# Two-layer gated-linear-attention and short-convolution trunk: the recurrence in 128-frame, two-head units with both chunks side by side on TensorE

## The chip, the cores and the metric

The kernel runs as one program on the 8 cores of one Trainium2 chip, one batch element a core. The metric is device time of the slowest core in microseconds (us). Every program here has a second, slower state: in some executions the cores of one die, or of both, get a lower granted TensorE clock and the time is some per cent longer. Below, "tile" means one pass of 512 frames through a mixer or a feed-forward; there are 8 of each in a layer and two layers, so 16 mixer tiles and 16 feed-forward tiles.

## The reference, cut to what matters

```python
def step(state, inp):                       # one chunk of 64 frames, 4 heads
    q_i, kd_i, v_i, g_i = inp
    state = g_i[..., None] * state + jnp.einsum('bhlk,bhlv->bhkv', kd_i, v_i)   # 128 x 256 a head
    o_i = jnp.einsum('bhlk,bhkv->bhlv', q_i, state)      # reads the state after its own chunk
    return state, o_i
# per layer
#   o   -> per-head RMSNorm, times silu(r), projection w_oa
#   conv: y_b = (gb_in * causal_depthwise_conv3(gc_in * cx)) @ w_ob
#   x  += (sigmoid(ga) * y_a + sigmoid(gb) * y_b) @ w_o
#   x  += SwiGLU(RMSNorm(x))
```

The state is float32. Shapes are x: 8 x 4096 x 1024; 4 heads with keys of 128 and values of 256; 64 chunks in sequence.

## The kernel before

A mixer tile computes q, k, v and the output gate, then runs the recurrence generator against the convolution generator, one step ("group") of each in turn. A group of the convolution is one accumulation of eight 128x512 matmuls, some 1.73 us, and the recurrence slips its small matmuls between them. 512 frames are four steps `ts` of 128 frames, each with two chunks `c`, nine groups a step.

```python
def AB(ts, c):                      # state matmuls of one chunk: all four heads, banks 2 and 3
    pr = slice(c * 64, (c + 1) * 64)
    for hp in range(2):
        mms([BK(2 + hp)], [... kd[pr, ts, head], v_s[pr, ts, head] ... for h2 in range(2)])
    for hh in range(4):             # VectorE: S = gamma * S + update, in place
        op("dve", [...], ["S32", ...], ... scalar_tensor_tensor(out=S32[:, hh, :], in0=S32[:, hh, :], ...))
    op("act", ["S32"], [("S16", si)], ...)          # ScalarE: one bf16 cast of all four heads
def C(ts, c): ...                   # output matmuls: q (64 frames) against the cast state
# E1: squares on ScalarE, rsqrt on GpSimd; E2: norm x gate on VectorE; Tr: eight transposes, two copies on VectorE
for ts in range(NTS):
    g = 9 * ts
    put(g, AB, ts, 0); put(g + 3, AB, ts, 1); put(g + 5, C, ts, 0); put(g + 6, C, ts, 1)
    put(g + 6, E1, ts); put(g + 9, E2, ts); put(g + 13, Tr, ts)
# ... (cut)
yield from interleave(gen_gla(), gen_conv(), [1])      # 41 groups of recurrence beside convolution
```

Beside a tile, the norm of the *next* tile starts a fixed number of groups in, and the weight casts to bf16 (DMAs that GpSimd issues, needed in the first layer for blocks of later stages) are paced by a rule:

```python
side += [lead(8), pre(), lead(8 if kind == "ffn" else 38), norm_h(s + 1)]
# ...
todo = casts.get(s, [])
ngroups = 52 if kind == "ffn" else 95
for _ in (mixer if kind == "mix" else ffn)(s):
    gi += 1
    next(sg, None)                                   # one step of the norm of the next tile
    while todo and gi * (len(casts[s]) + 1) > ngroups * (len(casts[s]) - len(todo) + 1):
        cast_piece(*todo.pop(0))
```

Of the kernel before, what the change touches and what calls it, by code (L numbers as in the profile page):

```python
# [12 lines left out]
KC = 8  # L13
# [112 lines left out]
def _mixer_blocks():  # L126

    c = _cols()
    w = lambda n, o, k: ("w_in", c[n] + o, k)
    bl = [("fzq", 8, 640, [w("fz", 0, 16)] * 8 + [w("q", 0, 512)])]  # L130
    bl += [("v0", 8, 512, [w("v", 0, 512)])]
    bl += [("k", 8, 512, [w("k", 0, 512)])]
    bl += [("v1", 8, 512, [w("v", 512, 512)])]
    bl += [("r%d" % h, 8, 512, [w("r", h * 512, 512)]) for h in range(2)]
    bl += [("cv%d" % i, 8, 640, [w(n, i * 128, 128) for n in ("C", "X", "B", "ga", "gb")]) for i in range(8)]
    bl += [("ab%d" % i, 8, 512, [(n, i * 256, 256) for n in ("w_oa", "w_ob")]) for i in range(4)]
    bl += [("o%d" % h, 8, 512, [("w_o", h * 512, 512)]) for h in range(2)]
    return bl
# [13 lines left out]
def build_nc(S):  # L152
# [19 lines left out]
    with ExitStack() as es:  # L172
# [9 lines left out]
        S32 = sb("S32", [128, 4, 256], F32)  # L182
        S16 = [sb("S16_%d" % i, [128, 4, 256], BF16) for i in range(2)]
        halo = sb("halo", [128, KC, 2], F32)
        gam = sb("gam", [128, 4, 2 * NTS], F32)
        ss = [sb("ss%d" % i, [128, 4], F32) for i in range(2)]
        rs2 = [sb("rs2_%d" % i, [128, 4], F32) for i in range(2)]
# [37 lines left out]
        ogtok = [carve([1024], BF16, "mix", [("og", i)]) for i in range(2)]  # L225
        ogT = carve([KC, T], BF16, "mix", R2("ogT", NTS, 2))
# [4 lines left out]
        ao[0] = span[("ogT", 0, 0)][1]  # L231
# [136 lines left out]
        def norm(xb, out_op):  # L368

            for j in range(4):  # L370
                i = min(j, 1)
                op("act", [("xT", xb, 2 * j), ("xT", xb, 2 * j + 1)], [("sq", i)],
                   lambda h, j=j, i=i: h.activation(out=sq[i][:], in_=xT[xb][:, 2 * j:2 * j + 2, :], func=AF.Square))  # L373
                if j:
                    op("dve", [("sq", 0), ("sq", 1)], [("sq", 0)],
                       lambda h: h.tensor_tensor(out=sq[0][:], in0=sq[0][:], in1=sq[1][:], op=ALU.add))  # L376
# [58 lines left out]
        def mixer(s):  # L435
# [6 lines left out]
            if t == 0:  # L442
                op("dve", [], ["S32"], lambda h: h.memset(S32[:], 0.0))
                op("dve", [], ["halo"], lambda h: h.memset(halo[:], 0.0))
# [79 lines left out]
            ei = 0  # L524
            for hf in range(2):
                sl, wk, w = get_block("r%d" % hf)
                for ts in range(NTS):
                    b = bank()
                    tm_group(b, w, wk, ts, h_, hk)
                    ei = 1 - ei  # L530
                    op("act", [BK(b)], ["eb%d" % ei], lambda h, b=b, ei=ei: h.activation(out=eb[ei], in_=pb[b][:, :], func=AF.Sigmoid))  # L531
                    op("dve", [BK(b), "eb%d" % ei], [("grs", ts, hf), BK(b)],
                       lambda h, b=b, ts=ts, hf=hf, ei=ei: h.tensor_tensor(out=grs[:, ts, hf * 512:(hf + 1) * 512], in0=pb[b][:, :], in1=eb[ei], op=ALU.mult))  # L533
                    yield
                done_block(sl)

            def gen_gla():
                s16c = [0]

                def AB(ts, c):  # L540
                    pr = slice(c * 64, (c + 1) * 64)
                    for hp in range(2):
                        ubk = 2 + hp
                        mms([BK(ubk)], [(mm(pb[ubk][:, h2 * 256:(h2 + 1) * 256], kd[pr, ts, (hp * 2 + h2) * 128:(hp * 2 + h2 + 1) * 128],
                                            v_s[pr, ts, (hp * 2 + h2) * 256:(hp * 2 + h2 + 1) * 256], True, True),
                                         [("kd", ts), ("v", ts, hp)]) for h2 in range(2)])
                    for hh in range(4):
                        ubk = 2 + hh // 2
                        op("dve", [BK(ubk), ("gam", hh)], ["S32", BK(ubk)],
                           lambda h, ubk=ubk, hh=hh, ts=ts, c=c: h.scalar_tensor_tensor(  # L550
                               out=S32[:, hh, :], in0=S32[:, hh, :], scalar=gam[:, hh, 2 * ts + c:2 * ts + c + 1],
                               in1=pb[ubk][:, (hh % 2) * 256:(hh % 2 + 1) * 256], op0=ALU.mult, op1=ALU.add))
                    si = s16c[0] % 2
                    s16c[0] += 1
                    op("act", ["S32"], [("S16", si)], lambda h, si=si: h.activation(out=S16[si][:], in_=S32[:], func=AF.Copy))  # L555

                def C(ts, c):
                    pr = slice(c * 64, (c + 1) * 64)
                    si = (ts * 2 + c) % 2
                    for hp in range(2):  # L560
                        mms([BK(hp)], [(mm(pb[hp][pr, (hh % 2) * 256:(hh % 2 + 1) * 256],
                                           qT[:, hh, ts * 128 + c * 64: ts * 128 + (c + 1) * 64], S16[si][:, hh, :], True, True),
                                        [("qT", hh), ("S16", si)]) for hh in (2 * hp, 2 * hp + 1)])

                def E1(ts):
                    r = ts % 2
                    for hh in range(4):
                        op("act", [BK(hh // 2)], ["junk", ("ss", r, hh)],
                           lambda h, hh=hh, r=r: h.activation(out=junk, in_=pb[hh // 2][:, (hh % 2) * 256:(hh % 2 + 1) * 256],  # L569
                                                              func=AF.Square, accum_out=ss[r][:, hh:hh + 1]))  # L570
                    op("pool", [("ss", r, hh) for hh in range(4)], [("rs2", r)],
                       lambda h, r=r: h.tensor_scalar(out=rs2[r][:], in0=ss[r][:], scalar1=1.0 / 256, scalar2=EPS, op0=ALU.mult, op1=ALU.add))
                    op("pool", [("rs2", r), "mhalf"], [("rs2", r)],
                       lambda h, r=r: h.tensor_tensor(out=rs2[r][:], in0=rs2[r][:], in1=mhalf[:, 0:4], op=ALU.pow))

                def E2(ts):
                    r = ts % 2
                    for hh in range(4):
                        op("dve", [BK(hh // 2), ("rs2", r), ("grs", ts, hh // 2)], [("og", r), BK(hh // 2)],
                           lambda h, hh=hh, r=r, ts=ts: h.scalar_tensor_tensor(  # L580
                               out=ogtok[r][:, hh * 256:(hh + 1) * 256], in0=pb[hh // 2][:, (hh % 2) * 256:(hh % 2 + 1) * 256],
                               scalar=rs2[r][:, hh:hh + 1], in1=grs[:, ts, hh * 256:(hh + 1) * 256], op0=ALU.mult, op1=ALU.mult))

                def Tr(ts):
                    r, tb = ts % 2, 2
                    tb16 = pb[tb][:, :].bitcast(BF16)
                    mms([BK(tb)], [(lambda pe, vc=vc: pe.transpose(tb16[:, vc * 128:(vc + 1) * 128], ogtok[r][:, vc * 128:(vc + 1) * 128], ident16[:]),  # L587
                                    ["ident16", ("og", r)]) for vc in range(8)])
                    for par in range(2):
                        src = tb16.rearrange("p (a b c) -> p a b c", a=4, b=2)[:, :, par, :]  # L590
                        dst = ogT[:, :, ts * 128:(ts + 1) * 128].rearrange("p (a b) c -> p a b c", b=2)[:, :, par, :]
                        op("dve", [BK(tb), "pk"], [("ogT", ts, par), BK(tb)],
                           lambda h, src=src, dst=dst, par=par: h.tensor_scalar_mul(out=dst, in0=src, scalar1=pkc(96 + l * 2 + par)))
# [4 lines left out]
                for ts in range(NTS):  # L598
                    g = 9 * ts
                    put(g, AB, ts, 0)  # L600
                    put(g + 3, AB, ts, 1)
                    put(g + 5, C, ts, 0)
                    put(g + 6, C, ts, 1)
                    put(g + 6, E1, ts)
                    put(g + 9, E2, ts)
                    put(g + 13, Tr, ts)
                for g in range(41):
# [4 lines left out]
            def gen_conv():  # L612
                for cc in range(8):
# [9 lines left out]
                    op("act", ["halo"], [("ub", u)], lambda h, u=u, cc=cc: h.activation(out=ub[u][:, 0:2], in_=halo[:, cc, :], func=AF.Copy))  # L623
                    op("dve", [BK(b), ("tmp", u)], [("ub", u), BK(b)],
                       lambda h, b=b, u=u, csb=csb: h.tensor_tensor(out=ub[u][:, 2:T + 2], in0=pb[b][:, :], in1=csb[:], op=ALU.mult))  # L625
                    op("act", [("ub", u)], ["halo"], lambda h, u=u, cc=cc: h.activation(out=halo[:, cc, :], in_=ub[u][:, T:T + 2], func=AF.Copy))
                    cw = lambda j, cc=cc: pkc(32 + (l * 3 + j) * 8 + cc)
                    op("dve", [("ub", u), "pk"], [("tmp", 2 + u)],
                       lambda h, u=u, cc=cc, cw=cw, cacc=cacc: h.tensor_scalar(out=cacc[:], in0=ub[u][:, 2:T + 2], scalar1=cw(2), scalar2=pkc(80 + l * 8 + cc),  # L629
# [208 lines left out]
```

## Time and profile before

The median was 4867.46 us (4866.63, 4867.46 and 5444.5). The profile is of a run of 4876.38 us; its slowest core, core 3, spans 4875.2 us. A table of the stages of that core, from the starts of successive tiles:

| stage, core 3 | us |
|---|---|
| before the first mixer tile | 31.1 |
| first mixer tile | 217.7 |
| mixer tiles 1 to 7, layer one | 1318.3 |
| mixer tiles, layer two | 1448.4 (180.9 each in the steady state) |
| 16 feed-forward tiles | 1860.0 |

The profile names engines PE (TensorE matmuls), PEld (its weight loads), DVE (VectorE), ACT (ScalarE), POOL (GpSimd) and SP. `L324` is a line of the kernel; most matmuls come through one helper and share that line, so a matmul is told by its tiles. A number in square brackets after a timeline entry is the idle time of that engine before it, and after the arrow stands what ended the idle time. What ended an idle time is inferred by the profiler's reader from semaphore events, and can be wrong.

### The profile page before, as it was taken

The numbers are of one execution on the slowest core, as the hardware profiler recorded it, in microseconds if no ns is written. First come the engines' busy times: TensorE is split into PE (matmuls) and PEld (weight loads), VectorE is DVE, ScalarE is ACT, GpSimd is POOL, SyncE is SP. The second block draws the span as 40 slices with busy tenths as digits, with TensorE's granted clock in tenths as the row PEclk, the third lists the DMA queues.
The fourth block names the chain that finished last, engine by engine and source line by source line (L and its number), as shares of the span: only waits on it lengthen the run. The fifth ranks groups of instructions, "written<-read, shape, count | busy, mean of one in ns | idle before, by whom it ended". The sixth has DMA issues, their size and how long they took to land.

```text
span 4875.2 us, 62749 instructions; the slowest of 8 cores (4823.3 to 4875.2 us)
## 1 busy us (share of the span) xinstructions
PE 4664.7 (96%) x21840; PEld 2092.2 (43%) x21840; DVE 2173.2 (45%) x3425; ACT 1348.2 (28%) x2479; POOL 130.1 (3%) x210
## 2 busy tenths in 40 slices
PE   6899899999999999999999999999999999999998
PEld 2334344444444444444444444444444444444443
DVE  3535545645545222222235545546645633333332
ACT  2232323323322111211123323323323312222221
POOL 0000000000000000000000000000000000000000
PEclk9989999999999999999999999999999999999999
DMA  9975674584775755566554464454454455555552
GB/s 208 227 197 164 149 207 160 145 205 151 184 203 188 225 192 192 183 195 197 183 177 155 146 197 169 140 190 159 139 186 168 131 213 188 191 186 190 182 186 90
DMA packets 124195, 870.18 MB, mean 178 GB/s; under 512 B 14480, under 2 KB 14608, under 8 KB 47504
## 3 DMA queue, kind: packets, MB, share of 16 engines
q1 hardware_dynamic: 116928, 782.29, 46.9%
q0 software_dynamic: 5952, 81.27, 11.0%
q8 instruction: 182, 2.98, 0.2%
q10 hardware_dynamic: 1008, 2.62, 0.2%
q14 instruction: 125, 1.02, 0.1%
HBM read 856.94 MB, written 148.37 MB: 206 GB/s over the span
## 4 chain that ended last, share of the span: by engine, by line
PE 81%; DVE 7%; DMA 6%; issue 3%; ACT 2%; DVEq 0%; ACTq 0%; POOL 0%; SPq 0%; POOLq 0%
PE pb L324 78%; DMA sb_wsl<-sc_mix_cv 3%; DVE sb_S L550 2%; PE pb L336 2%; DMA sb_wsl<-w_mix 1%; DVE sb_arena L580 1%; ACT sb_sq L373 1%; DVE sb_tmp L633 1%; DVE sb_ub L625 1%; ACT sb_arena L569 1%; PE pb L587 1%; DMA sc_mix_cv<-sb_wsl 1%; DVE sb_tmp L629 1%; DVE sb_sq L376 0%; DMA sc_mix_k<-sb_wsl 0%
## 5 line engine op out<-in xcount | busy, mean ns | idle before, releaser
L324 PE MATMUL pb<-sb_hT,sb_wsl 128*128 128x512 bf16 x8768 | 2030.2, 389 | 40.4 <-DMA sb_wsl<-sc_mix_cv 30.3
L324 PEld LDWEIGHTS pb<-sb_hT,sb_wsl 128*128 128x128 bf16 x8768 | 848.9, 100 | 1119.8 <-issue 226.0
L324 PE MATMUL pb<-sb_arena,sb_wsl 128*128 128x512 bf16 x3836 | 837.2, 379 | 2.0 <-DMA sb_wsl<-w_mix 1.9
L324 PE MATMUL pb<-sb_hT,sb_arena 128*128 128x512 bf16 x3136 | 683.2, 379 | 0.0
L704 ACT ACTIVATE sb_tmp<-pb 128x512 f32<-128x512 f32 x352 | 209.8, 596 | 1300.6 <-PE pb L324 1255.4
L324 PEld LDWEIGHTS pb<-sb_arena,sb_wsl 128*128 128x128 bf16 x3836 | 374.3, 98 | 452.2 <-issue 5.0
L709 DVE TENSOR_TENSOR sb_arena<-pb,sb_tmp 128x512 bf16<-128x512 f32 x352 | 242.8, 690 | 683.5 <-PE pb L324 614.2
L324 PE MATMUL pb<-sb_arena 128*128 128x512 bf16 (+1 forms) x2052 | 420.7, 355 | 83.2 <-DVE sb_S L550 83.2
L324 PEld LDWEIGHTS pb<-sb_hT,sb_arena 128*128 128x128 bf16 x3136 | 307.2, 98 | 374.0 <-issue 7.4
L324 PE MATMUL pb<-sb_wsl,sb_hT 128*128 128x512 bf16 x2048 | 460.3, 384 | 4.6 <-DMA sb_wsl<-w_mix 4.6
L419 DVE TENSOR_TENSOR sb_xT<-pb,sb_xT 128x512 f32<-128x512 f32 x256 | 171.1, 689 | 648.2 <-PE pb L324 567.5
L324 PEld LDWEIGHTS pb<-sb_arena 128*128 128x128 bf16 (+1 forms) x2052 | 188.1, 97 | 329.4 <-issue 144.0
L324 PEld LDWEIGHTS pb<-sb_wsl,sb_hT 128*128 128x128 bf16 x2048 | 200.6, 99 | 245.1 <-issue 27.0
L550 DVE SCALAR_TENSOR_TENSOR sb_S<-sb_S,sb_gam,pb 128x256 f32<-128x256 f32 x512 | 245.0, 478 | 64.6 <-ACT sb_S_0 L555 22.3
L495 ACT ACTIVATE sb_arena<-pb 128x512 bf16<-128x512 f32 x64 | 36.2, 590 | 734.2 <-PE pb L324 734.2
L633 DVE SCALAR_TENSOR_TENSOR sb_tmp<-sb_ub,sb_pk,sb_tmp 128x512 f32<-128x512 f32 x256 | 192.3, 751 | 27.4 <-DVE sb_tmp L629 0.5
L625 DVE TENSOR_TENSOR sb_ub<-pb,sb_tmp 128x512 f32<-128x512 f32 x128 | 88.3, 690 | 253.9 <-ACT sb_ub L623 130.8
L376 DVE TENSOR_TENSOR sb_sq<-sb_sq 128x1024 f32<-128x1024 f32 x120 | 147.0, 1225 | 118.4 <-ACT sb_sq L373 96.9
L373 ACT ACTIVATE sb_sq<-sb_xT 128x1024 f32<-128x1024 f32 x160 | 166.7, 1051 | 104.5 <-DVE sb_sq L376 81.4
L401 DVE SCALAR_TENSOR_TENSOR sb_hT<-sb_xT,sb_pk,sb_rstd 128x512 bf16<-128x512 f32 x256 | 175.5, 745 | 31.5 <-ACT sb_rstd L386 31.5
L640 ACT ACTIVATE sb_arena<-pb 128x512 bf16<-128x512 f32 x256 | 148.4, 588 | 56.5 <-PE pb L324 55.9
L533 DVE TENSOR_TENSOR sb_arena<-pb,sb_arena 128x512 bf16<-128x512 f32 x128 | 87.1, 691 | 163.3 <-ACT sb_arena L531 159.2
(77 smaller groups left out, 2392.5 us busy)
## 6 DMA issues: line engine op xcount, KB each, us to landing
sb_wsl<-sc_mix_cv SPq DMA_DIRECT2D x120, 1280.0 KB, 7.2
sb_arena<-sc_ffn_f SPq DMA_DIRECT2D x98, 1024.0 KB, 5.7
sb_wsl<-sc_ffn_f SPq DMA_DIRECT2D x78, 1024.0 KB, 6.0
sb_wsl<-sc_mix_ab SPq DMA_DIRECT2D x60, 1024.0 KB, 5.0
sb_arena<-sc_ffn_d SPq DMA_DIRECT2D x70, 704.0 KB, 4.6
xs<-sb_xT SPq DMA_DIRECT2D x48, 1024.0 KB, 4.7
sb_xT<-xs SPq DMA_DIRECT2D x96, 512.0 KB, 8.3
sb_wsl<-sc_ffn_d SPq DMA_DIRECT2D x58, 704.0 KB, 4.8
```

The costliest lines, as they stand in the source:

```text
L324: return lambda pe: pe.matmul(out, lhsT, rhs, start=first, stop=last)
L336: ins = e.h.matmul(pb[b][:, :], w[:, kc, col0:col0 + 128], rhsT[:, kc, :], start=(kc == 0), stop=(kc == KC - 1))
L373: lambda h, j=j, i=i: h.activation(out=sq[i][:], in_=xT[xb][:, 2 * j:2 * j + 2, :], func=AF.Square))
L376: lambda h: h.tensor_tensor(out=sq[0][:], in0=sq[0][:], in1=sq[1][:], op=ALU.add))
L401: lambda h, kc=kc: h.scalar_tensor_tensor(out=hT[xb][:, kc, :], in0=xT[xb][:, kc, :], scalar=pkc(g0 + kc), in1=rstd[:], op0=ALU.mult, op1= ...
L419: lambda h, b=b, dc=dc: h.tensor_tensor(out=xT[xb][:, dc, :], in0=pb[b][:, :], in1=xT[xb][:, dc, :], op=ALU.add))
L550: lambda h, ubk=ubk, hh=hh, ts=ts, c=c: h.scalar_tensor_tensor(out=S32[:, hh, :], in0=S32[:, hh, :], scalar=gam[:, hh, 2 * ts + c:2 * ts + ...
L625: lambda h, b=b, u=u, csb=csb: h.tensor_tensor(out=ub[u][:, 2:T + 2], in0=pb[b][:, :], in1=csb[:], op=ALU.mult))
L633: lambda h, u=u, cw=cw, j=j, cacc=cacc: h.scalar_tensor_tensor(out=cacc[:], in0=ub[u][:, j:T + j], scalar=cw(j), in1=cacc[:], op0=ALU.mult ...
L640: lambda h, b=b, dst=dst, cc=cc: h.activation(out=dst[:, cc, :], in_=pb[b][:, :], func=AF.Sigmoid))
L704: lambda h, b=b, si=si: h.activation(out=tmp[si][:], in_=pb[b][:, :], func=AF.Silu))
L709: lambda h, b=b, si=si, fc=fc: h.tensor_tensor(out=hid[:, fc, :], in0=pb[b][:, :], in1=tmp[si][:], op=ALU.mult))
```

## The change

Its intent: take the recurrence's small matmuls closer together and its waits apart. The unit becomes 128 frames and two heads. Both chunks of a unit are issued alternately: state matmuls on TensorE's upper and lower 64 rows, output matmuls on its left and right 64 columns. Two are meant to run at once; for the column halves no run had shown it yet. A unit comes every six groups, 52 groups in all, and the output gate's projection and half of the convolution's output projection join the convolution as filler. The state alternates between two float32 buffers. Transpose copies and the first convolution tap go from VectorE to ScalarE, the halo copies from ScalarE to GpSimd. The norm of the next tile starts four groups earlier, and its four squares get one more group each (an added `yield`), so that its root and its multiplications still come at the same group count of the tile.

```diff
+                def AB(u):
+                    ts, hp = u // 2, u % 2
+                    mms([BK(0), BK(1)], [(mm(pb[c][:, h2 * 256:(h2 + 1) * 256],
+                                             kd[c * 64:(c + 1) * 64, ts, (hp * 2 + h2) * 128:(hp * 2 + h2 + 1) * 128],
+                                             v_s[c * 64:(c + 1) * 64, ts, (hp * 2 + h2) * 256:(hp * 2 + h2 + 1) * 256], True, True),
+                                          [("kd", ts), ("v", ts, hp)]) for h2 in range(2) for c in range(2)])
 ... (four state updates on VectorE, S32[c] -> S32[1 - c])
+                def SC(u):            # one bf16 cast on ScalarE per chunk, two heads
+                def C(u):             # four output matmuls, h2 outer, c inner, one bank; squares, rsqrt
-                for ts in range(NTS):
-                    g = 9 * ts
-                    put(g, AB, ts, 0)
 ... (cut)
+                for u in range(8):
+                    for d, st in ((0, AB), (1, SC), (3, C), (6, E2), (9, Tr)):
+                        put(6 * u + d, st, u)
+                for g in range(52):
 ... (convolution)
-                    op("act", ["halo"], [("ub", u)], ... halo copy in ...)
+                    op("pool", [("halo", cc)], [("ubh", u)], ... halo copy in ...)
-                    op("dve", [("ub", u), "pk"], [("tmp", 2 + u)], ... first tap ...)
+                    op("act", [("ub", u), "pk"], [("tmp", 2 + u)], ... first tap ...)
 ... (cut)
+            def main():
+                yield from gen_r()
+                yield from gen_conv()
+                yield from gen_ob(0)
-            yield from interleave(gen_gla(), gen_conv(), [1])
+            yield from interleave(gen_gla(), main(), [1])
 ... (cut)
-                side += [lead(8), pre(), lead(8 if kind == "ffn" else 38), norm_h(s + 1)]
+                side += [lead(8), pre(), lead(8 if kind == "ffn" else 34), norm_h(s + 1)]
 ... (in the norm, after each of the four squares)
+                yield
```

## The prediction

> **What bounds the kernel now.** I read the summary of engines first, then TensorE's waits, then the timeline of one undisturbed mixer tile, then stretches.
>
> ```profile
> PE 4664.7 (96%) x21840; PEld 2092.2 (43%) x21840; DVE 2173.2 (45%) x3425; ACT 1348.2 (28%) x2479; POOL 130.1 (3%) x210
> ```
>
> TensorE is the bound; the other engines matter only where they make it wait. Of its matmuls, 19840 are bf16 with 512 columns. At full clock they start 215.8 ns apart in the trace, so they cost 19840 x 0.2158 = 4281 us, and the change touches none of them. A stretch of a feed-forward tile shows that floor with nothing on top:
>
> ```profile
> core 7: us, PE busy (x) PEld busy (x) DVE busy (x) ACT busy (x) POOL busy (x), PEclk, DMA share, GB/s
> 1550.00:1663.00 113.00, 113.00 (x524) 51.19 (x522) 29.36 (x41) 22.31 (x31) 0.58 (x1) 1.00 0.73 247
> ```
>
> Differences between the starts of successive tiles put the 16 feed-forward tiles together at 1860.0 us on all eight cores, the 16 mixer tiles at 2934 to 2984 us, with 31 us ahead of the first mixer. In the second layer every mixer tile takes 180.8 to 181.0 us on every core. The waits say what is in a mixer beyond matmuls (us in total, times, longest):
>
> ```profile
> PE pb L324 <- DVE sb_S L550: 83.2, 35, 12.3
> PE pb L587 <- DVE sb_S L550: 34.9, 19, 2.3
> PE pb L324 <- DMA sb_wsl<-sc_mix_cv: 30.3, 5, 9.9
> PE pb L324 <- DVE sb_sq L379: 28.9, 2, 21.0
> ```
>
> The first two, 118 us, are the recurrence: a matmul needs a PSUM bank that VectorE's state update (L550) has not yet emptied, or a transpose needs the normalised output. The fourth is 21 us of start and 8 us of the last norm. One second-layer tile of core 7 in TensorE's timeline:
>
> ```profile
> 2898.82 1.90 PE L324 MATMUL pb<-sb_hT,sb_wsl 128*128 128x512 bf16 x8
> 2903.01 1.00 PE L587 MATMUL pb<-sb_ident,sb_arena 128*128 128x128 bf16 x8 [2.29 <-DVE sb_S L550]
> 2903.80 3.21 PE L324 MATMUL pb<-sb_hT,sb_wsl 128*128 128x512 bf16 x8
> ...
> 2934.62 5.35 PE L324 MATMUL pb<-sb_hT,sb_wsl 128*128 128x512 bf16 x24
> 2943.64 0.38 PE L324 MATMUL pb<-sb_arena 64*128 64x256 bf16 x2 [3.67 <-DVE sb_S L550]
> 2944.81 0.58 PE L324 MATMUL pb<-sb_arena 64*128 64x256 bf16 x2 [0.79 <-DVE sb_S L550]
> 2945.32 3.60 PE L324 MATMUL pb<-sb_hT,sb_wsl 128*128 128x512 bf16 x8
> ```
>
> Each tile has two stalls, at the first output transpose and where the last 128 frames meet the next tile's norm on VectorE, 6.7 us together; after each, eight matmuls take 3.2 to 3.6 us instead of 1.9, because the clock was halved. The first tile has another limit:
>
> ```profile
> 60.00:110.00 50.00, 42.15 (x198) 18.25 (x195) 15.97 (x26) 16.07 (x32) 2.11 (x4) 0.97 1.01 231
> 180.00:230.00 50.00, 45.55 (x209) 20.36 (x208) 29.81 (x46) 5.50 (x16) 3.92 (x6) 0.97 1.01 218
> ```
>
> The last two numbers are the share of the DMA engines and GB/s (core 3): weights are read, cast and stored there, and the queues are full. Later mixer tiles of core 7 have shares of 0.54 to 0.69.
>
> [...] the four forget-gate matmuls of 16 rows start 7 ns apart, and their eight f32 passes occupy about 1.07 us together. No run here shows it for column groups yet. [...] a full matmul followed by a 64-row one is 311 ns from start to start instead of 215, and the first full one after a 64-row one comes 202 ns after its start instead of 109. [...] the change gives the two chunks banks 0 and 1. [...]
>
> **The change part by part, for a steady mixer tile.**
>
> *Pairing.* Before, eight calls of four state matmuls (64 rows, 256 columns) cost 311 - 216 = 95 ns to enter, 3 x 109, and 202 to leave: 0.62 us each, and eight output calls (64 columns) the same: 94 + 327 + 205 = 0.63. After, there are again eight of each with four matmuls, but alternating between two groups, so a call is two rounds of 109 instead of four: about 95 + 218 + 93 + some 10 ns = 0.42 us. Saving 0.21 x 16 = 3.3 us a tile. The mode switches stay; the 32 transposes stay at 56 ns.
>
> *The recurrence's stalls.* Before, 128 frames pass in nine groups, state steps three groups apart, each step updating four heads (4 x 0.478 us) in two banks that the next step needs. The recurrence is spread over 41 groups with convolution alone, whose VectorE work I sum per tile as 32 x 0.478 updates, 16 x 0.482 gates, 8 x 0.482 transpose copies, 8 x (0.690 + 0.547 + 2 x 0.751 + 0.686) convolution and 10 us of norm: 65 us of some 81 without stalls. After, a unit comes every six groups (6 x 1.73 = 10.4 us plus about 1.1 of its own), and transpose copies and the first tap go to ScalarE: 52 groups hold some 65 us of VectorE work, the output gates' products and four more included, in about 97 us. The state banks have six groups to be emptied, not three. State values alternate between two buffers, so an update no longer waits for the cast of the one before.
>
> The tightest path left is state matmul to output matmul, three groups apart, about 5.6 us. In it: a leftover convolution operation, at worst two taps until 1.4 us; two output gates, to 2.5; four updates at 0.58 spacing, to 4.7; the second half-size cast, to some 5.4 (estimated 0.63 from 1.06 for the double size). So it just fits, and with a norm addition (1.23 us) inside it misses by about a microsecond. I allow 1.5 us of small stalls a tile[...].
>
> *Halo copies to GpSimd.* VectorE waited 130.8 us in total for ScalarE's tiny copy of the two carried frames (L623), which stood behind state casts in ScalarE's order. That wait leaves with its order; it was one source of the stalls above, so I count it once.
>
> *Sum.* 712 x 0.2158 = 153.7; state and output calls 16 x 0.42 = 6.8; output transposes 1.8; key transposes 0.9; forget gate 1.2; norm sum 0.9. That is 165.3, plus 1.5: 166.8 us against 180.8, or 14 less: 3.3 of pairing, 6.7 of stalls less the 1.5 that remain, and the rest, about 5.5, the halved clock after them and smaller waits.
>
> *First layer.* The first tile, 209 to 218 us, is full of DMA; its 12.35 us stall comes from GpSimd, which stood at a weight load (behind the store of an earlier block) with the normalisation behind it. That order stays, now with the halo copies behind it too. I keep 213. Tiles 1 to 7 stall up to 9.9 us for a convolution block, when casts for later layers share the DMA engines. Those loads stay. Convolution blocks will be used up every 9.4 us instead of 11, so I keep 40 us for these seven tiles rather than the 35 that core 7 shows.
>
> Total: 31 + 213 + (7 x 166.8 + 40) + (8 x 166.8 + 2) + 1860 = 4648 us in the profile. The timed runs were 9 us below the profile before (4867 against 4876), so 4640.
>
> **Rivals.** (1) *Column groups do not overlap*: half of the pairing goes, 8 x 0.21 x 16 = 27 us more, 4667. For it: narrow weight loads average 112 ns in the trace, longer than the 98 of full ones, and nothing before shows two column groups together. Against it: loads overlap matmuls everywhere else. (2) *The wait only moves*: output matmuls or transposes wait for casts on ScalarE, which now also has copies and the first tap (estimate 128 x 0.6 + 256 x 0.38 = 174 us more on 1348), or VectorE waits for GpSimd. At 3 us a tile with a halved clock behind it, that is 16 x 5 = 80 us more, 4720. For it: the tight path above and table loads of 1.28 us around the norm. Against it: ScalarE stays near 1500 us. (3) *DMA becomes the bound in the first layer*: blocks come late at the faster pace; 7 x 5 = 35 us more, 4675. Against it: shares of 0.54 to 0.69. (4) *All stalls vanish*, first tile included: 4640 - 24 - 25 = about 4590.
>
> **Range and chances.** Pairing and stalls would both have to fail for 2% (97 us) to be missed; even rival 2 leaves 3%. The range goes from just above rival 4 to short of rival 2: 4598 to 4700. Faster by over 2%: 0.97; within 2%: 0.025; slower: 0.005.
>
> **What would show it.** In the profile after: feed-forward tiles unchanged; second-layer mixer tiles at 165 to 169 us; VectorE state waits on TensorE below 40 us in total instead of 118; four state matmuls in about 0.3 us from first start to last end of streaming, and a few nanoseconds between starts of a pair, also for the column pairs; less half clock than the 215 us of core 3 before; convolution-block waits still there. It would be wrong if second-layer tiles stay above 172 us, with a wait on casts (ScalarE) or on GpSimd in place of L550.

## The result, and the profile after

The changed kernel is correct. Its first four runs took 4721.24 us (fast) and 5055.97, 5084.69 and 4960.37 us (slow), two more 4729.34 us (fast) and 5074.42 us (slow). The ratio of fast runs to those of before is 0.971 (95% interval 0.9682 to 0.9738): faster, by 141 us. Ratios here and below are the mean time of one kernel's fast runs over that of the other's of the same rounds, so not quite the ratio of the medians quoted. The kernel was run again later (see the experiments): 4719.62, 4723.27 and 4726.6 us, ratio 0.9705. The profile is of the run of 4721.24 us, and the sums below are against it: the predicted 4640 us is 81 us too low, and the range ended 21 us below it.

The summary of engines and TensorE's waits after (core 3, the slowest; us in total, times, longest) answer to the first and third fence of the prediction:

```profile
PE 4549.9 (96%) x21840; PEld 2035.9 (43%) x21840; DVE 2026.7 (43%) x3169; ACT 1535.9 (33%) x2735; POOL 226.3 (5%) x594
```

```profile
PE pb L324 <- DMA sb_wsl<-sc_mix_cv: 47.3, 7, 11.0
PE pb L324 <- DVE sb_sq L380: 29.4, 2, 21.4
PE pb L324 <- ACT sb_S_2 L561: 21.5, 16, 1.4
PE pb L591 <- DVE sb_arena L582: 18.5, 19, 14.0
PE pb L324 <- DMA sb_wsl<-w_mix: 18.2, 11, 2.8
PE pb L324 <- ACT sb_S_3 L561: 11.6, 16, 1.0
```

The 83.2 + 34.9 us of waits on VectorE's state update (L550 before) are gone. In their place stand waits on ScalarE's cast of the last unit (sb_S_2 and sb_S_3, L561): 21.5 and 11.6 us, each sixteen times, that is once in every mixer tile. The convolution block wait grew from 30.3 to 47.3 us.

The pairs do overlap. Four output matmuls of one call in the timeline (start, duration, engine, line, tiles):

```profile
1024.19 0.30 PE L324 MATMUL pb<-sb_S_0,sb_arena 128*64 128x256 bf16 x1
1024.20 0.30 PE L324 MATMUL pb<-sb_S_1,sb_arena 128*64 128x256 bf16 x1
1024.33 0.27 PE L324 MATMUL pb<-sb_S_0,sb_arena 128*64 128x256 bf16 x1
1024.33 0.27 PE L324 MATMUL pb<-sb_S_1,sb_arena 128*64 128x256 bf16 x1
```

The two chunks (S_0 and S_1) start within 10 ns of each other, and the second pair 130 ns later. The starts of a state call pair in the same way: at the median 3 ns between the two starts of a pair and 116 ns from pair to pair (core 3). Medians over all calls, from the start of the matmul before the call to the start of the one after it, less the time that its kind takes from start to start (0.216 us, after a transpose 0.056), are 0.42 us for a state call and about 0.44 for an output call, against 0.64 and 0.65 before.

A steady mixer tile of the second layer takes 170.3 us, against 180.9 before and 166.8 predicted. What keeps it above 166.8 is one place in the tile. Core 3, timeline, cut to what leads to the wait:

```profile
3028.81 1.28 ACT L386 ACT_TABLE_LOAD   x1
...
3030.84 0.69 DVE L623 TENSOR_TENSOR sb_ub<-pb,sb_tmp 128x512 f32<-128x512 f32 x1 [2.65 <-ACT sb_rstd L386]
...
3031.42 1.02 ACT L597 ACTIVATE sb_arena<-pb,sb_pk 128x256 bf16<-128x256 bf16 x2
...
3033.28 0.80 ACT L627 ACTIVATE sb_tmp<-sb_ub,sb_pk 128x512 f32<-128x512 f32 x1
...
3034.87 1.61 DVE L633 SCALAR_TENSOR_TENSOR sb_tmp<-sb_ub,sb_pk,sb_tmp 128x512 f32<-128x512 f32 x2 [1.84 <-POOL sb_ub L621]
...
3036.40 2.73 DVE L402 SCALAR_TENSOR_TENSOR sb_hT<-sb_xT,sb_pk,sb_rstd 128x512 bf16<-128x512 f32 x4
3039.05 1.07 DVE L582 SCALAR_TENSOR_TENSOR sb_arena<-pb,sb_rs_0,sb_arena 128x256 bf16<-128x256 f32 x2
...
3040.03 1.05 DVE L552 SCALAR_TENSOR_TENSOR sb_S_1<-sb_S_0,sb_gam,pb 128x256 f32<-128x256 f32 x2
...
3041.18 0.63 ACT L561 ACTIVATE sb_S_2<-sb_S_1 128x512 bf16<-128x512 f32 x1 [4.71 <-DVE sb_S_1 L552]
...
3041.95 0.27 PE L324 MATMUL pb<-sb_S_2,sb_arena 128*64 128x256 bf16 x1 [1.42 <-ACT sb_S_2 L561]
...
3042.93 0.27 PE L324 MATMUL pb<-sb_S_3,sb_arena 128*64 128x256 bf16 x1 [0.70 <-ACT sb_S_3 L561]
...
3043.24 5.09 PE L324 MATMUL pb<-sb_hT,sb_wsl 128*128 128x512 bf16 x15
```

Read from the top. The norm of the next tile (its table load of 1.28 us, L386, L387, and its multiplications L402) meets the last unit of the recurrence. The first idle time of VectorE, 2.65 us, is put down to the norm's root (L386), but that is a coincidence of times: L623 does not read the root, and it started 0.18 us after its own convolution group had ended on TensorE, as 80 of the 128 L623 of this core did. VectorE merely had no work. The second is real: 1.84 us for the halo copy of GpSimd (L621), which comes behind two small operations (L574, L576) that wait for ScalarE's squares, and these stand behind the norm's root on ScalarE. Then the convolution taps, four norm multiplications (2.73 us) and two output gates all go ahead of the state updates, which begin at 3040.03. The state matmuls had been issued at 3034.05, so the updates come 6 us after them, and the casts behind: ScalarE had stood idle for 4.71 us until the update came. TensorE loses 1.42 + 0.70 us, and the chunks of this unit run one after the other instead of in pairs. Behind it the clock is halved (granted 0.50 from 3043.25 to 3046.66): 15 matmuls take 5.09 us, where at 0.2158 us a start they would take about 3.4. The stretches of that tile (us, busy time and count of each engine, granted clock, DMA share, GB/s) put a size to it:

```profile
2923.50:3093.90 170.40, 168.01 (x836) 75.05 (x835) 91.90 (x150) 71.43 (x137) 12.41 (x34) 0.99 0.54 175
3041.90:3050.00 8.10, 7.34 (x28) 3.02 (x29) 4.19 (x7) 4.69 (x11) 1.06 (x3) 0.79 0.01 2
```

TensorE idles 170.40 - 168.01 = 2.4 us in the tile, and in the 8.1 us around the wait the mean clock of 0.79 costs 8.1 x 0.21 = 1.7 us more. With the pairing that this one call lost, these are most of the 4.9 us by which the tile stands above the 165.4 that experiments below reach. The record holds a check of the 1.7 us: on every core one second-layer tile takes 168.6 or 168.7 us instead of 170.3, and on core 3 (its tile 2) that one has the same waits of 1.42 and 0.70 us (2873.36 and 2874.33) and no halved clock: the granted clock is 1.00 from 2868 to 2876, and the 24 matmuls behind take 5.35 us. The other seven second-layer tiles of that core each have one stretch of half clock, 3.41 us long. What spared the eighth is not shown; the same stall cost 2.1 us there and about 3.8 in the others.

In the first layer, tiles 1 to 7 of core 3 took 180.0, 180.2, 173.8, 170.9, 181.8, 180.4 and 181.9 us: 57 us above seven steady ones. The first tile took 216.5 us and the feed-forward tiles 1860.1. The sum is 31.5 + 216.5 + 1249.0 + 1363.1 + 1860.1 = 4720.2 us.

### The profile page after: what moved, and what is told of

It is laid out like the page before. It is cut to its first block, busy times and chain, and to the rows that moved or that the text cites.

```text
span 4720.2 us, 63804 instructions; the slowest of 8 cores (4686.8 to 4720.2 us)
## 1 busy us (share of the span) xinstructions
PE 4549.9 (96%) x21840; PEld 2035.9 (43%) x21840; DVE 2026.7 (43%) x3169; ACT 1535.9 (33%) x2735; POOL 226.3 (5%) x594
## 2 busy tenths in 40 slices
DMA packets 124202, 870.25 MB, mean 184 GB/s; under 512 B 14480, under 2 KB 14608, under 8 KB 47504
## 4 chain that ended last, share of the span: by engine, by line
PE 85%; DMA 9%; DVE 2%; ACT 2%; issue 1%; POOL 0%; ACTq 0%; DVEq 0%; POOLq 0%; SPq 0%
PE pb L324 83%; DMA sb_wsl<-sc_mix_cv 4%; DMA sb_wsl<-w_mix 3%; PE pb L336 2%; DVE sb_hT L402 1%; DMA sc_mix_cv<-sb_wsl 1%; ACT L386 0%; PE pb L591 0%; DMA sc_mix_r<-sb_wsl 0%; DMA sc_mix_fzq<-sb_wsl 0%; DMA sc_mix_oa<-sb_wsl 0%; DVE sb_S_1 L552 0%; DVE sb_S_0 L552 0%; DVE sb_tmp L633 0%; ACT sb_arena L571 0%
## 5 line engine op out<-in xcount | busy, mean ns | idle before, releaser
L324 PE MATMUL pb<-sb_hT,sb_wsl 128*128 128x512 bf16 x8768 | 1983.5, 384 | 60.4 <-DMA sb_wsl<-sc_mix_cv 47.3
L725 DVE TENSOR_TENSOR sb_arena<-pb,sb_tmp 128x512 bf16<-128x512 f32 x352 | 243.3, 691 | 783.2 <-PE pb L324 652.1
L324 PE MATMUL pb<-sb_arena 128*128 128x512 bf16 (+1 forms) x2052 | 386.8, 353 | 0.0
L324 PEld LDWEIGHTS pb<-sb_arena 128*128 128x128 bf16 (+1 forms) x2052 | 165.1, 97 | 232.4 <-issue 49.6
L402 DVE SCALAR_TENSOR_TENSOR sb_hT<-sb_xT,sb_pk,sb_rstd 128x512 bf16<-128x512 f32 x256 | 177.9, 746 | 31.7 <-ACT sb_rstd L387 30.1
L623 DVE TENSOR_TENSOR sb_ub<-pb,sb_tmp 128x512 f32<-128x512 f32 x128 | 88.3, 690 | 224.4 <-PE pb L324 139.6
L647 DVE TENSOR_TENSOR sb_arena<-pb,sb_tmp 128x512 bf16<-128x512 f32 x128 | 88.0, 687 | 166.8 <-PE pb L324 166.8
L597 ACT ACTIVATE sb_arena<-pb,sb_pk 128x256 bf16<-128x256 bf16 x256 | 119.9, 469 | 112.8 <-PE pb L591 100.7
```

What stands on the lines that cost most here:

```text
L324: return lambda pe: pe.matmul(out, lhsT, rhs, start=first, stop=last)
L402: lambda h, kc=kc: h.scalar_tensor_tensor(out=hT[xb][:, kc, :], in0=xT[xb][:, kc, :], scalar=pkc(g0 + kc), in1=rstd[:], op0=ALU.mult, op1= ...
L597: lambda h, src=src, dst=dst, par=par: h.activation(out=dst, in_=src, func=AF.Copy, scale=pkc(96 + l * 2 + par)))
L623: lambda h, b=b, u=u, csb=csb: h.tensor_tensor(out=ub[u][:, 2:T + 2], in0=pb[b][:, :], in1=csb[:], op=ALU.mult))
L725: lambda h, b=b, si=si, fc=fc: h.tensor_tensor(out=hid[:, fc, :], in0=pb[b][:, :], in1=tmp[si][:], op=ALU.mult))
```

## The experiments

Eleven runs in three series on three chips. The fast runs of the kernel before were 4870.26 to 4878.36 us in the first series, a single 4878.02 in the second (so no ratios there) and 4863.19 to 4872.9 in the third. Edits are against the changed kernel unless the text says otherwise. "Tile" is the steady mixer tile of the second layer.

### Halo copy earlier (e1_halo_early)

The first theory put the late state update down to GpSimd's halo copy, which ended the 1.84 us wait. Here it is issued one group earlier.

```diff
                     csb, cacc = tmp[u], tmp[2 + u]
+                    op("pool", [("halo", cc)], [("ubh", u)], ... tensor_copy(out=ub[u][:, 0:2], in_=halo[:, cc, :]))
                     b = bank()
 ... (one group)
-                    op("pool", [("halo", cc)], [("ubh", u)], ... tensor_copy(out=ub[u][:, 0:2], in_=halo[:, cc, :]))
```

> Edit: GpSimd's copy of the carried frames into the convolution buffer is issued one matmul group earlier, ahead of the normalisation of the same turn. Theory A (GpSimd's order): in the changed kernel VectorE stands still for 1.84 us at 3034.87 because that copy waits in GpSimd's queue behind the normalisation, which waits for ScalarE; this delays the state updates and is what makes the output matmul of the last unit wait 1.42 + 0.70 us and halves the clock. Then the wait of TensorE for the state casts (L561) falls from 33 us to below 15 us in total, steady second-layer mixer tiles go from 170.3 to 166 to 167 us, the whole from 4721 to about 4660 (fast runs). Theory B (the norm's own work on VectorE, eight scalings and the wait for the inverse root, fills the path whatever GpSimd does): tiles stay at 169.5 to 170.5 us and the whole within 10 us of 4721.

Measured: 4707.38 and 4709.39 us fast, ratio 0.9662 (0.9638 to 0.9685); tile 167.9 to 169.9. That is 13 us better than the changed kernel, between the ranges of the two theories, but the wait on the casts is still there 33 times, 32.9 us in total. The timeline of core 3 at the same place:

```profile
3029.96 1.61 DVE L633 SCALAR_TENSOR_TENSOR sb_tmp<-sb_ub,sb_pk,sb_tmp 128x512 f32<-128x512 f32 x2 [1.50 <-ACT sb_tmp L627]
```

VectorE now waits 1.50 us at the same instruction, for the first tap on ScalarE (L627) instead of the halo copy (the tap had ended 0.46 us before; what held the rest isn't in the trace). The 13 us are mostly half clock that did not come: in the second layer of core 3 every tile still has its 2 us of waits, but only four of eight have a halved clock behind them (169.6 us and more) where the changed kernel has it in seven; the others take 167.9 to 168.2 (mean granted clock of the cores 0.987 to 0.990, against 0.986 to 0.988). The theory that the halo copy was the cause fell: it was the last of several things that come late together, all behind ScalarE's work for the norm.

### First tap back on VectorE as well (e8_tap_dve)

```diff
-                    op("act", [("ub", u), "pk"], [("tmp", 2 + u)], ... activation(..., scale=cw(2), bias=...))
+                    op("dve", [("ub", u), "pk"], [("tmp", 2 + u)], ... tensor_scalar(..., op0=ALU.mult, op1=ALU.add))
```
(on top of the earlier halo copy)

> Edit: as e1 (GpSimd's copy earlier), and the first convolution tap is back on VectorE. In e1 the wait only changed its name: VectorE stood 1.50 us for that tap on ScalarE, which had a table load, the two steps of the inverse root, two transpose copies and two squares ahead of it in its order, and the stall of 1.42 + 0.71 us stayed. Theory F (the work moved to ScalarE closes the chain norm, ScalarE, VectorE, state casts): with the tap on VectorE (0.55 us of work instead of 1.50 us of waiting) the state updates of the last unit come about 0.95 us earlier; the wait for casts falls from 2.1 to some 1.2 us a tile, TensorE's clock is not halved in second-layer tiles, these take 166.5 to 167.5 us, the whole about 4670. Theory B (the norm's eight scalings on VectorE are what fills the path): stall of 2 us and tiles of 168 to 170 as in e1.

Measured: 4699.8 and 4700.03 us fast (four of six runs were slow); tile 168.0, half a microsecond above what was expected, and the whole 30 us above it. No halved clock is left in the second layer's mixers (mean granted clock of the cores 0.989 to 0.992 over the run), but TensorE still waits for the casts 29.1 us in total, now in 50 pieces (in one tile of core 0 0.39, 0.55 and 0.71 us). VectorE has no wait left at that place, and the updates still start 4.5 us after their state matmuls, behind the norm's multiplications. So each of the two edits removes one way of being late and the next takes its place; the crowd itself stays.

### The norm nine groups later (e2_late_norm)

If the crowd is the cause, moving the norm past the last unit removes it at once.

```diff
-                side += [lead(8), pre(), lead(8 if kind == "ffn" else 34), norm_h(s + 1)]
+                side += [lead(8), pre(), lead(8 if kind == "ffn" else 43), norm_h(s + 1)]
```

> Edit: the next tile's norm starts nine groups later, so that its scalings on VectorE fall behind the last unit's state updates. Both theories of e1 say that the stall goes, since A and B both need the norm inside a unit: tiles at 165.5 to 167 us, the whole near 4650. Theory C (ScalarE has too much to do with the work moved to it, wherever the norm is): some unit still waits for its casts in every tile, tiles stay at 169 us or more, whole at 4700 or more.

Measured: 4659.97, 4660.13, 4660.65 and 4677.62 us fast, ratio 0.9572 (0.9548 to 0.9595). Tile 165.4. The waits of the profiled run's slowest core, and a whole second-layer tile of it, engines in the same order as above:

```profile
PE pb L324 <- DMA sb_wsl<-sc_mix_cv: 42.6, 7, 11.0
...
PE pb L324 <- ACT sb_S L561: 1.9, 2, 1.3
```

```profile
2800.00:2965.00 165.00, 165.00 (x833) 74.13 (x832) 90.92 (x149) 69.01 (x135) 10.92 (x35) 1.00 0.54 180
```

The cast wait went from 33 us to 1.9, TensorE is busy for 165.00 of 165.00 us at a clock of 1.00, and VectorE's work in the tile is the same as before the edit (90.92 us in 165, against 91.90 in 170.4). One number settles the cause: the meeting of norm and last unit, not the amount of work on any engine. Some 61 us came off the whole.

### Weight casts evenly over the tile (e4_even_casts)

The pacing rule uses the length of a list that it empties: with n casts left the next is due at group 95/(n + 1), so five casts come at groups 16, 20, 24, 32 and 48, not evenly. Here the length is fixed at the start.

```diff
-            ngroups = 52 if kind == "ffn" else 95
+            ngroups = 52 if kind == "ffn" else 86
+            ncast = len(todo)
-                while todo and gi * (len(casts[s]) + 1) > ngroups * (len(casts[s]) - len(todo) + 1):
+                while todo and gi * (ncast + 1) > ngroups * (ncast - len(todo) + 1):
```

> Edit: the weight casts for later layers are issued at equal distances over a mixer tile; as it stands the list shrinks while it is counted and three of five fall between groups 16 and 24. Theory D (bunched casts delay the convolution blocks of first-layer tiles 1 to 7, which take 57 us more than seven steady ones on core 3): TensorE's wait for convolution blocks falls from 47 us to below 15, these seven tiles lose 30 to 45 us, the whole goes to about 4685. Rival E (the DMA engines are short in total there, so the time of a cast does not matter): wait stays above 35 us and the whole within 10 us of 4721.

Measured: 4669.54 and 4691.43 us fast, ratio 0.9604 (0.9564 to 0.9645). Tile 170.3, unchanged. Tiles 1 to 7 of the first layer are 168.6 to 171.7 us on every core, and the convolution block wait has left the list of waits. On core 3 these seven tiles lost 55 us (1249 to 1194), more than the 30 to 45 expected. Two stretches of the sixth mixer tile (t = 5), first the changed kernel (core 3), then this one (core 2):

```profile
983.00:1013.00 30.00, 24.40 (x124) 10.45 (x122) 15.31 (x28) 15.16 (x30) 3.33 (x9) 0.99 1.10 155
1013.00:1043.00 30.00, 24.63 (x119) 10.58 (x120) 10.38 (x19) 10.25 (x23) 3.01 (x9) 0.84 0.77 225
```

```profile
963.00:993.00 30.00, 30.00 (x156) 13.25 (x155) 16.31 (x30) 16.87 (x33) 3.07 (x9) 1.00 0.82 199
993.00:1023.00 30.00, 30.00 (x156) 13.26 (x155) 15.98 (x28) 17.55 (x37) 5.05 (x13) 1.00 0.66 173
```

In the changed kernel three casts were issued within 16 us (980.96, 988.74 and 996.52), the DMA share reaches 1.10, TensorE loses 11 us in the two stretches and then runs at a clock of 0.84. Here the casts are 26 to 31 us apart, the shares are 0.82 and 0.66, and TensorE is busy throughout. The bytes are the same (870.25 MB in both). So it was the bunching of the casts, not the pace of the tile or the amount of DMA.

### Order of the four matmuls (e3_no_alternation)

Does the alternation of the two chunks make the pairs?

```diff
-    ... for h2 in range(2) for c in range(2)])
+    ... for c in range(2) for h2 in range(2)])        # both state and output calls
```

> Edit: the four matmuls of a state or output call in the order chunk, head instead of head, chunk[...]. If the pairs really run at once (starts 3 to 7 ns apart in the trace of the changed kernel), a call has three rounds of 109 ns instead of two: 0.11 us x 16 calls x 16 tiles = 28 us more, about 4749 in fast runs, steady tiles 172.0. If the recorded starts mislead and a pair takes the time of two, nothing changes (4721).

Measured: one fast run of six, 4729.66 us; tile 170.3, unchanged. The expected loss of 28 us, the estimate for a third round of 109 ns a call, did not come. A state call and an output call of core 0:

```profile
2961.47 0.39 PE L324 MATMUL pb<-sb_arena 64*128 64x256 bf16 x4
...
2967.09 0.41 PE L324 MATMUL pb<-sb_S,sb_arena 128*64 128x256 bf16 x4
```

Four matmuls still fit in 0.39 and 0.41 us from the first start to the last modelled end, as in the changed kernel (medians 0.39 and 0.41, core 3), while the instruction stream has two of one chunk and then two of the other. The records do not carry which of the four each is, so how they share the array in this order is not shown; that the order makes no difference to the time is. Before, four matmuls of one chunk in a call started 119, 109 and 109 ns apart and took 0.61 us from first start to last end. The shorter calls came with both chunks in one call, in either order.

### Units every five groups, less filler (e5_no_spread)

Does the spread over 52 groups, with output gates beside it, buy anything?

```diff
-                        put(6 * u + d, st, u)
-                for g in range(52):
+                        put(5 * u + d, st, u)
+                for g in range(45):
 ... (gen_r() out of main(), run ahead of the interleave instead)
```

> Edit: the changed kernel with a unit every five groups instead of six, beside convolution and the first four output projections only; the output gates come ahead, as in the kernel before. Theory S (the spreading is what removed the large stalls): state updates collide more often, tiles at 173 us or more, whole at 4765 or more. Theory P (pairing, two banks for a whole unit and alternating state buffers did it; the spreading is not needed): tiles at 170 to 172 us, of which some 1.3 us is the wait of the output projection for the last transposes, whole 4720 to 4750.

Measured: 4681.81, 4683.19 and 4715.13 us fast; tile 166.3 us. The denser recurrence is *faster* than the spread one by 4 us a tile, and its waits on casts are 18.2 us, of which 13.6 are one wait in the first tile. The norm meets the recurrence here too, but in another phase, as a second-layer tile of core 3 shows:

```profile
3017.15 2.73 DVE L402 SCALAR_TENSOR_TENSOR sb_hT<-sb_xT,sb_pk,sb_rstd 128x512 bf16<-128x512 f32 x4
...
3019.06 0.39 PE L324 MATMUL pb<-sb_arena 64*128 64x256 bf16 x4
...
3021.72 2.04 DVE L552 SCALAR_TENSOR_TENSOR sb_S<-sb_S,sb_gam,pb 128x256 f32<-128x256 f32 x4
```

The four norm multiplications are nearly done when the last unit's state matmuls start, so its updates begin 2.7 us behind these instead of 6; the unit before loses 0.25 us. Spreading is therefore not what removed the stalls of the kernel before. The six-group spacing of the change happens to set its last unit into the norm's burst.

### The norm later in the kernel before (e9_before_late_norm)

This one is the kernel before, with its lead of 38 made 47.

> Edit: the kernel before, with nothing changed but the norm nine groups later. It asks how much of the loss of the kernel before was the meeting of norm and recurrence alone. The stall of 3.67 + 0.79 us and the halved clock behind it (some 3 us) should go; the one at the first transpose (2.29 us and some 1.5 us) should stay: tiles at 173 to 175 us instead of 180.8, whole about 4760. If the meeting with the norm only hides another stall at the same place: 178 us or more, whole above 4830.

Measured: 4784.59, 4785.36 and 4786.2 us fast; tile 174.0 to 174.4. The tile is as expected and the whole 25 us above it, because the convolution block waits of the first layer stay (tiles 1, 2, 5 and 6 of core 3 are 186 to 188 us). The waits on the state update, over the whole span of core 0, its slowest:

```profile
PE pb L587 <- DVE sb_S L550: 40.5, 37, 2.6
PE pb L324 <- DVE sb_S L550: 37.3, 37, 11.8
```

One number takes 82 us off the kernel before (93 against the one fast run of its own series), more than half of what the change takes. In a steady tile the waits went from 6.9 to 4.6 us and the halved clock from 10.2 us (5.1 lost) to none. The norm's stall of 3.67 + 0.79 us shrank to 0.69 + 0.80; the one of 2.29 us at the first transpose stayed, but on that core no half clock followed it (mean granted clock 0.988 over the span, 0.977 on that core before). Why none followed is not shown, so the 1.7 us that it had cost before (half of 3.41) are not shown to be the norm's. With the norm moved in both kernels the change is worth 4785 - 4660 = 125 us (from two series), or 174.2 - 165.4 = 8.8 us a tile.

### All three edits, and without the halo copy (e6_all_three, e11_best_again, e12_late_even, e13_after_again)

> Edit: the changed kernel with the norm nine groups later, casts at equal distances and GpSimd's copy earlier. If the two losses that e2 and e4 took away are independent, steady tiles take 165.4 us in both layers, tiles 1 to 7 of the first layer within 2 us of that, and the whole is 31 + 217 + 15 x 165.4 + 1.3 + 1860 = about 4590 us. If the faster tiles run into the DMA queues again, it stays near 4640.

Measured: one fast run of six, 4596.79 us. The profile fell in the slow state with one die undisturbed: there tiles are 165.4 us in both layers. On the other die, where the granted clock averages 0.887 over the span, a mixer tile at the lower clock takes 200.3. One fast run called for a repetition, and the edits for a separation:

> The kernel with all three edits (norm nine groups later, casts evenly over the tile, halo copy one group earlier) again, for more fast runs. If its one fast time was representative: 4585 to 4610 us fast, steady second-layer mixer tile 165.3 to 165.6 us on an undisturbed die, tiles 1 to 7 of the first layer under 168 us.

> Late norm and even casts without the earlier halo copy. Late norm alone gave a tile of 165.4 us, which is the sum without stalls, so the halo copy should have nothing left to save: 4597 us, within 10 us of the kernel with all three, tile 165.4 us. If GpSimd's halo copy still costs, the tile is 166 us or more and the time 4605 to 4625.

> The changed kernel, unaltered, because its own series had one fast run in four. If that run was representative: fast runs of 4715 to 4730 us, ratio to the kernel before near 0.970, steady second-layer mixer tile 170.3 us. A time near 4690 or 4700 would mean that the prediction's range held and that the cause looked for is smaller than 72 us in the profile.

Measured, in one series: all three edits 4593.54, 4594.34, 4595.47 and 4596.36 us fast, ratio 0.9441 (0.9427 to 0.9456), with all eight cores at a mean granted clock of 0.994 or 0.995. Late norm and even casts alone: 4595.48 us, its one fast run of six. The changed kernel unaltered: 4719.62, 4723.27 and 4726.6 us. The expectations held (that profile of the unaltered kernel is of a slow run; its undisturbed die shows the tile of 170.3). The halo edit has nothing left to save once the norm is out of the way. The summary of the kernel with two edits, and its largest waits (core 7):

```profile
PE 4510.4 (98%) x21840; PEld 2027.8 (44%) x21840; DVE 2019.4 (44%) x3169; ACT 1504.3 (33%) x2705; POOL 207.3 (5%) x594
```

```profile
PE pb L324 <- DVE sb_sq L380: 29.3, 2, 21.4
PE pb L324 <- DMA sb_wsl<-w_mix: 15.4, 9, 3.5
PE pb L591 <- DVE sb_arena L582: 13.9, 1, 13.9
...
PE pb L324 <- ACT sb_S L561: 2.6, 3, 1.3
```

These are the start of the program and the last norm (21.4 and 7.9 us), the direct weight loads, and one wait of 13.9 us in the first mixer tile. The first tile, 209 to 221 us with its DMA engines full (share 1.01 before and in the changed kernel, core 3), moved in no experiment; nothing here tried to move it.

## Why the prediction was right or wrong

The difference of 81 us between 4640 and 4721.24 adds up by the prediction's own terms, against core 3 of the profile after:

| term of the sum | predicted | measured | difference |
|---|---|---|---|
| before the first mixer tile | 31 | 31.5 | 0.5 |
| first tile | 213 | 216.5 | 3.5 |
| tiles 1 to 7, steady part | 7 x 166.8 | 7 x 170.3 | 24.5 |
| tiles 1 to 7, DMA waits | 40 | 56.9 | 16.9 |
| second layer | 8 x 166.8 + 2 | 1363.1 | 26.7 |
| feed-forward | 1860 | 1860.1 | 0.1 |
| timed run against profile | -8 | +1.0 | 9.0 |

**Right: the matmuls.** The sum without stalls, 165.3 us a tile, is the tile of every kernel without the collision: 165.4. That covers pairing, mode switches (312 ns from the last full matmul to the first of a state call, against 216 between full ones) and transposes. (The calls before were 0.02 us longer than its 0.62 and 0.63: their first two starts are 119 and 133 ns apart, not 109.) The column pairs overlap as the row pairs do (0.41 and 0.39 us from first start to last end of four, 0.62 and 0.61 before), so rival 1 did not happen. The feed-forward did not move. The waits named after VectorE's state update went from 118 us to none, but in name only: the casts that TensorE waits for now were themselves waiting for the update. The halved clock on core 3 fell from 215 to 128.8 us.

**Wrong, and the largest part: "I allow 1.5 us of small stalls a tile".** No half clock was allowed for behind them. Measured were about 2.4 us of waiting and a halved clock behind it: 4.9 us above the tile without stalls, 3.5 above the allowance, some 51 us over the run. The prediction had named the place: the path from state matmul to output matmul, which "just fits, and with a norm addition (1.23 us) inside it misses by about a microsecond". It took 7.9 us (3034.05 to 3041.95) instead of 5.6. Before the updates stood not one addition but four norm multiplications (2.73 us), and ahead of them VectorE was still held by the halo copy for 0.8 us of its 1.84 after the state matmuls had started. In the timeline that hold is a chain over three engines: VectorE waited 1.84 us for GpSimd's copy, which came behind two operations that waited for ScalarE's squares, and these came after the norm's root. Without any such hold (e8_tap_dve) the multiplications alone still make the casts late. The prediction summed VectorE's work over 52 groups and found it ample; it was ample (e2_late_norm has the same work and no stall), but a sum over a tile cannot show where two bursts meet. To allow for no half clock was wrong as well: its own profile before had one behind a stall of 2.29 us (core 7, granted 0.50 from 2903.06 to 2906.47). How long a stall is did not decide it alone: the same 1.42 and 0.70 us had half clock behind them in seven second-layer tiles of core 3 and none in the eighth. What else decides is not shown.

**Rival 2 came nearest.** It described a wait that moves to ScalarE's casts, or to VectorE waiting for GpSimd, at 5 us a tile with the halved clock, 4720 us in all. Both forms are in the timeline. Its first form holds for the name of the wait alone: ScalarE's added work did not delay the cast, for ScalarE stood idle 4.71 us before it. The second, VectorE waiting for GpSimd, was there, but taking it away left the stall (e1_halo_early). That its 4720 us met 4721.24 is luck in part: this stall makes 51 of the 81 us, and the rest comes from terms that rival 2 did not touch. The evidence that the prediction set against it, a total of ScalarE work near 1500 us, was right too (1535.9) and says nothing of where the waits fall. The chance given to rival 2 was too small, and the range was drawn to end short of it.

**Wrong: "I keep 40 us for these seven tiles".** 56.9 on core 3. The size was taken from core 7, where it came out right (40.1), but the time is the slowest core's; the cause, casts that share the DMA engines with convolution blocks, was right, and the bunched pacing rule was in the code to be read. Even pacing takes the waits away wholly, with no fewer bytes.

**Wrong: "The timed runs were 9 us below the profile".** The profiled run of before had itself taken 4876.38 us. It was set by core 3, which had a spell of the lower clock (0.8125 for 153 us; its tile 1 took 205.4 us, that of core 7 191.1); the slowest core without one spans 4867.7. So the 9 us belong to that run, not to profiling, and the sum, which has no such spell in it, should not have been lowered by them.

**Half right: where the gain came from.** The prediction put 6.7 us a tile down to stalls, less those that remain, and credited the spread over 52 groups. The kernel before with only its norm moved gains 6.7 us (180.9 to 174.2): the halved clock cost 5.1 us less there and the waits 2.3 less (0.7 of that is not found in the gain), so these losses, too, were mostly the norm's, but for the 1.7 us named above. Units every five groups (166.3) show that the spread itself wasn't needed. What the change brings of its own, 8.8 us a tile, is by the traces about 3.4 of pairing (sixteen calls, each 0.21 us shorter), the 4.6 us of waits that the kernel before keeps with its norm moved, and a rest of 0.8. Which part of the change takes these waits away was not separated.

## What to carry to other kernels

Before trusting a sum of work per tile, lay out in time what each engine has queued at the tightest point of the chain; two bursts that meet there (here a norm and the last step of a recurrence) cost what no total shows, and moving one by a few steps may be worth half of the redesign or more. When a change shifts the schedule, search again for the offsets that were set for the old one: one number made 61 us here, and a pacing rule another 52. Test such an offset on the old kernel as well, or its gain is booked to the redesign. And before a few microseconds of gain are put down to an edit, look whether a halved clock has come or gone (here 1.7 us a tile, with the same waits before it).
